# Linear attention's scores two levels at a time in mid-chunk, and its outputs in a lane of their own

## The chip, the cores and the metric

The kernel runs on one core of a Trainium2 chip. The time is that of one execution on the device, in microseconds. Five engines work side by side, each through its own queue of instructions in order: TensorE (PE in the profile, its weight loads PEld), VectorE (DVE), ScalarE (ACT), GpSimd (POOL) and SyncE (SP), which starts the DMAs. TensorE writes to PSUM, which here is two pools of four banks.

## The reference

Two layers of an encoder over 256 tokens and 16 learned meta tokens in front, width 2048. Each layer makes one large projection of the stream (6176 columns), two groups of attention heads from it, an output projection, a layer norm, a squared-ReLU MLP (width 8192) and a second layer norm. The meta tokens are dropped from the output.

The part that the change touches is the four heads of gated linear attention (query and key width 128, value width 256). Its recurrence, in each of the two directions, is

```
S_t = diag(a_t) S_{t-1} + k_t^T v_t        o_t = q_t S_t        log a_t = gate <= 0
```

and the head's output is normalised by its own mean square, scaled, and multiplied by SiLU of a gate that is also projected from the stream. The eight pairs of heads of neighbourhood attention, over a 4 x 64 grid with a window, a learned bias and the meta tokens as further keys, are interleaved with it.

## The kernel before, in words

*The stream of projections.* Everything large is a matmul with weights from HBM. A weight tile of 128 x 1024 is fetched (`raw`), rounded to fp32r on ScalarE (`wh`, L147) and its remainder is made by one subtraction on VectorE (`wl`, L148), so that two fp32r numbers stand for one fp32 number; the activations are kept in two parts as well. `three` (L151 on) makes each product of three matmuls, or of two where the right operand's halves lie side by side. `by_m` makes one output chunk of 128 columns at a time: 16 steps over the width, weights for 8 steps per tile, so a chunk takes two weight tiles. Weights are asked for one tile ahead, and `raw`, `wh` and `wl` have three buffers each.

*Where the small work goes.* The small work of the mixers is written as Python generators. They stand in two lanes, `fg` and `bg`. After every weight tile, that is in the middle and at the end of each output chunk, `by_m` calls `pump`, which lets the generators run on: one step of `fg`, and so many steps of `bg` as a credit allows. The credit grows by `GLA_R` = 1.3 per pump while the gates' eight chunks are projected, and by `GLA_NA` = 1.1 while the neighbourhood attention's 24 chunks are. The steps are issued behind the last weight's subtraction on its engine (`issue_after(self.wl)`), and the framework's scheduler sets the final order on each queue.

*Linear attention.* `gla_head` is one generator for one head; the four heads stand in `bg` one behind the other. The decay between two tokens is split by binary levels: at each level the sequence is cut in blocks, and the exponent is taken against the middle of the block, so that no exponent is positive. For each of the levels 7, 0, 1, ... 6, 8 `operands` makes four subtractions on GpSimd (L462), one exponential on ScalarE (L467) and one product with q and k on VectorE (L468). Then come the score matmuls: four of 64 x 64 (L497), for level 8 two of 128 x 128 (L492), and in the first layer one small one for the meta tokens (L500) at levels up to 4. The result is copied or written under a mask into `A`, `near` and `Am` (L503 to L518). `across` does the same for the meta tokens against all others (L522, L525). One level is made ready while the one before it is used; the levels' tile `lev` has three buffers. Then the same generator makes `am`, the output matmuls in two halves (L540 to L542), the mean square by two fp32r matmuls against a matrix of 1/256 (`mean`, L774), a Newton step for the inverse root (L432 to L434), and the normalised, gated outputs in two parts (L558, L559, `split`). Each head has 17 steps. The scores and outputs are plain fp32; projections and means are fp32r.

*Beside it.* `silu` makes the gates: the reciprocal on VectorE in two halves (L422), one per step, and the product in a third. `na_pair` is one generator per pair of attention heads in `fg`: it fetches the bias into `nb`, makes the scores (L599, L603), adds, softmaxes, transposes the values (L620, L621), then the probabilities (L635 to L638), and makes the outputs (L650, L655). After five of the six groups of attention projections `layer` runs `bg` empty and closes the pool of the linear attention.

*Banks.* Projections take PSUM banks from the pool `pm`, all the small work from `pb`.

Of the kernel before, what the change touches and what calls it, by code (L numbers as in the profile page):

```python
# [7 lines left out]
F32 = mybir.dt.float32  # L8
# [3 lines left out]
ALU = mybir.AluOpType  # L12
PSUM = bass.MemoryType.PSUM

P = 128
# [19 lines left out]
GLA_R, GLA_NA, NORMS = 1.3, 1.1, (1.0, 0.6)  # L35
# [12 lines left out]
class Trunk:  # L48
    def __init__(self, ctx, tc, ins, out):
        self.ctx, self.tc, self.nc = ctx, tc, tc.nc  # L50
        self.i, self.out = ins, out
        self.bg, self.fg, self.credit, self.fcredit = deque(), deque(), 0, 0
# [11 lines left out]
    def bank(self):  # L64
        return self.pb.tile([P, 512], F32, name="bg", tag="bg")
# [38 lines left out]
    def pump(self, fg, bg):  # L104
        self.fcredit += fg
        while self.fcredit >= 1:
            self.step(self.fg, 1)
            self.fcredit -= 1
        self.credit += bg
        while self.credit >= 1:  # L110
            self.step(self.bg, 1)
            self.credit -= 1

    def drain(self):
        while self.bg or self.fg:
            self.step(self.bg, 1)
            self.step(self.fg, 1)
# [72 lines left out]
    def by_m(self, acts, ns, evict, pump=(0, 0), apart=False, renew=False):  # L190

        nk = len(acts)
        for m, n in enumerate(ns):
            ps = self.pm.tile([P, 512], F32, name="mm", tag="mm")
            for k in range(nk):
# [3 lines left out]
                if k % 8 == 7 and k < nk - 1:  # L199
                    self.pump(*pump)  # L200
# [4 lines left out]
            self.pump(*pump)  # L205
# [16 lines left out]
    def layer(self, l):  # L222
# [4 lines left out]
        with ExitStack() as actx:  # L227
# [10 lines left out]
            if l:  # L238
                self.by_m(self.x, [L + 2] * 4, lambda m, ps: self.fixed(self.ev_k, m, ps), pump=(1, NORMS[0]),
# [9 lines left out]
            with ExitStack() as ectx:  # L249
                self.ep = pool("early", "right", ectx)  # L250
                self.fcredit = 0
                self.fg.append(self.gates())
                if l == 0:
                    self.by_m(self.x, [L] * 4, self.ev_v, pump=(1, 0))
                else:
                    for m, ps in enumerate(first):
                        self.ev_v(m, ps)
                self.by_m(self.x, [n] * 4, self.ev_q, pump=(1, 0))
                self.by_m(self.x, [L] * 4, lambda m, ps: self.ev_v(4 + m, ps), pump=(1, 0))
                self.drain()  # L260
            self.a2 = pool("na", "left", bufs=2)
            with ExitStack() as gctx:
                self.credit = 0
                self.g2 = pool("gla", "right", gctx, 2)
                for h in range(GH):
                    self.bg.append(self.gla_head(h))
                for g in range(2):
                    self.by_m(self.x, [n] * 4, lambda m, ps: self.ev_r(4 * g + m, ps), pump=(1, GLA_R))
                self.na_tiles()
                for g in range(6):  # L270
                    if g == 5:
                        while self.bg:
                            self.step(self.bg, 1)
# [3 lines left out]
                    self.by_m(self.x, ns, lambda m, ps: self.ev_na(4 * g + m, ps), pump=(1, GLA_NA))  # L277
# [140 lines left out]
    def silu(self, c, s, r):  # L418
        yield
        half = self.n // 2  # L420
        for p in (slice(0, half), slice(half, self.n)):
            self.nc.vector.reciprocal(s[:, p], s[:, p])  # L422
            yield
# [12 lines left out]
    def gla_head(self, h):  # L436
        nc, n, full, g2 = self.nc, self.n, self.full, self.g2
        be, qk = self.be[h], self.qk[h]
        bf, eb = be[:, 0, :], be[:, 1, :]
        A = g2.tile([P, 6, P], F32, name="A", tag="A")  # L440
        near = g2.tile([P, 2, 64], F32, name="near", tag="near")
        Am = g2.tile([NM, L], F32, name="Am", tag="Am")
        level = lambda: g2.tile([P, 2, L], F32, name="lev", tag="lev", bufs=3)

        def flat(t):

            return t.rearrange("p a c -> p (a c)")

        def operands(lv):
            if lv == 0:  # L450
                q2 = level()[:, 1, :]
                nc.gpsimd.tensor_scalar(q2[:, :n], qk[:, 1, :n], 2.0, 0.0, ALU.mult, ALU.add)
                return q2, flat(qk)
            w = L if full and lv <= 4 else T
            B, hb = 1 << lv, 1 << (lv - 1)
            nb = w // B
            t = level()
            v = lambda a: a[:, :w].rearrange("p (b h) -> p b h", h=B)
            f, e, tq, tk = v(bf), v(eb), v(t[:, 1, :]), v(t[:, 0, :])
# [7 lines left out]
            nc.scalar.activation(t[:, :, :w], t[:, :, :w], AF.Exp, scale=1 / TAU)  # L467
            nc.vector.tensor_tensor(t[:, :, :w], t[:, :, :w], qk[:, :, :w], ALU.mult)  # L468
            return t[:, 1, :], flat(t)

        def across():
            t = level()
            bm, e0 = bf[:, L - 1:L], eb[:, 0:1]
            ts = nc.gpsimd.tensor_scalar
            ts(t[:, 1, :T], bf[:, :T], bm, 1.0, ALU.subtract, ALU.mult)
            ts(t[:, 0, T:L], bf[:, T:L], bm, -1.0, ALU.subtract, ALU.mult)
            ts(t[:, 1, T:L], eb[:, T:L], e0, -1.0, ALU.subtract, ALU.mult)
            ts(t[:, 0, :T], eb[:, :T], e0, 1.0, ALU.subtract, ALU.mult)
            nc.scalar.activation(t, t, AF.Exp, scale=1 / TAU)
            nc.vector.tensor_tensor(t[:, 1, :n], t[:, 1, :n], qk[:, 1, :n], ALU.mult)  # L480
            nc.vector.tensor_tensor(t[:, 0, :], t[:, 0, :], qk[:, 0, :], ALU.mult)
            return t

        order = (7, 0, 1, 2, 3, 4, 5, 6, 8)
        ahead = operands(order[0])
        for at, lv in enumerate(order):
            q, k = ahead
            ahead = operands(order[at + 1]) if at + 1 < len(order) else across()
            ps = self.bank()
            for s in range(2):  # L490
                if lv == 8:
                    nc.tensor.matmul(ps[:, s * P:s * P + P], lhsT=k[:, s * P:s * P + P],  # L492
                                     rhs=q[:, P - s * P:T - s * P], start=True, stop=True)
                    continue
                for b in range(2):
# [525 lines left out]
```

## Time and profile before

| what | value |
|---|---|
| median of 3 runs | 2424.95 us (2424.75 to 2425.05) |
| the profiled execution's own time | 2424.98 us |
| its span, first to last instruction | 2423.2 us |
| granted TensorE clock | 0.997 |
| busy: PE / DVE / ACT / POOL | 2392.5 / 1575.1 / 1191.2 / 290.6 us |
| DMA | 417 MB, mean 172 GB/s |

The profile describes one execution. A line such as `L497 PE MATMUL bg<-lev 128*64 128x64 f32 x448` names the source line, the engine, the operation, the tile written and the tiles read, the part of the array that is used (rows * columns), the moving operand's shape, and how many there were. A plain fp32 matmul of the program appears as two in the profile. Numbers behind a bar are busy time, mean duration in ns, and the engine's idle time just before with what ended it. A row of the waits says who waited for whom: us in total, how often, the longest. A row of the timeline gives start and duration in us; matmuls overlap, so the distance between two starts says more of their price than the durations do. A row of windows gives the stretch, its length, busy time and number of instructions of PE, PEld, DVE, ACT and POOL, the clock, the DMA share and GB/s.

### The profile page before, as it was taken

The numbers are of one execution on the slowest core, as the hardware profiler recorded it, in microseconds if no ns is written. First come the engines' busy times: TensorE is split into PE (matmuls) and PEld (weight loads), VectorE is DVE, ScalarE is ACT, GpSimd is POOL, SyncE is SP. The second block draws the span as 40 slices with busy tenths as digits, with TensorE's granted clock in tenths as the row PEclk, the third lists the DMA queues.
The fourth block names the chain that finished last, engine by engine and source line by source line (L and its number), as shares of the span: only waits on it lengthen the run. The fifth ranks groups of instructions, "written<-read, shape, count | busy, mean of one in ns | idle before, by whom it ended". The sixth has DMA issues, their size and how long they took to land.

```text
span 2423.2 us, 43590 instructions
## 1 busy us (share of the span) xinstructions
PE 2392.5 (99%) x17532; PEld 2259.4 (93%) x17532; DVE 1575.1 (65%) x2481; ACT 1191.2 (49%) x1978; POOL 290.6 (12%) x447
## 2 busy tenths in 40 slices
PE   9999999999999999999999999999999999999997
PEld 8999999999999999999999889999988888888886
DVE  6678777775544455546577787778866555666655
ACT  6555555564433344444456555555644333444443
POOL 1165320010000000000020444300200000000000
PEclk9999999999999999999999999999999999999998
DMA  7544445555555555555546445446556555665553
GB/s 240 166 131 152 141 138 157 174 175 178 174 177 175 174 174 174 174 175 174 175 168 187 146 146 158 145 155 192 184 190 187 188 190 185 189 188 186 188 188 129
DMA packets 118361, 417.26 MB, mean 172 GB/s; under 512 B 13388, under 2 KB 16460, under 8 KB 118160
## 3 DMA queue, kind: packets, MB, share of 16 engines
q1 hardware_dynamic: 118160, 414.49, 54.6%
q8 instruction: 137, 2.24, 0.4%
q14 instruction: 64, 0.52, 0.1%
HBM read 412.34 MB, written 2.10 MB: 171 GB/s over the span
## 4 chain that ended last, share of the span: by engine, by line
PE 93%; DVE 3%; POOL 1%; issue 1%; ACT 1%; DMA 0%; SPq 0%; ACTq 0%; POOLq 0%; DVEq 0%
PE mm L156 22%; PE mm L160 17%; PE mm L162 17%; PE mm L161 17%; PE mm L157 11%; PE mm L186 5%; POOL lev L462 1%; DVE wl L148 1%; PE bg L497 1%; DVE acc L866 1%; PE bg L650 1%; PE bg L599 0%; PE bg L540 0%; PE bg L323 0%; PE bg L541 0%
## 5 line engine op out<-in xcount | busy, mean ns | idle before, releaser
L148 DVE TENSOR_TENSOR wl<-raw,wh 128x1024 fp32r<-128x1024 f32 (+1 forms) x772 | 946.9, 1227 | 656.0 <-ACT wh L147 646.4
L147 ACT CAST wh<-raw 128x1024 fp32r<-128x1024 f32 (+1 forms) x772 | 805.2, 1044 | 952.0 <-PE mm L161 403.5
L160 PE MATMUL mm<-x,wh 128*128 128x272 f32 (+2 forms) x2176 | 632.3, 291 | 0.0
L162 PE MATMUL mm<-x,wl 128*128 128x272 f32 (+2 forms) x2176 | 628.0, 289 | 0.0
L161 PE MATMUL mm<-x,wh 128*128 128x272 f32 (+2 forms) x2176 | 627.8, 288 | 0.0
L160 PEld LDWEIGHTS mm<-x,wh 128*128 128x128 f32 x2176 | 412.7, 190 | 3.2 <-issue 0.4
L162 PEld LDWEIGHTS mm<-x,wl 128*128 128x128 f32 x2176 | 410.1, 188 | 0.3
L156 PE MATMUL mm<-x,wh 128*128 128x512 f32 x1152 | 409.5, 397 | 0.0
L161 PEld LDWEIGHTS mm<-x,wh 128*128 128x128 f32 x2176 | 409.4, 188 | 0.0
L157 PE MATMUL mm<-x,wl 128*128 128x256 f32 x1152 | 324.6, 282 | 0.4 <-DVE wl L148 0.4
L156 PEld LDWEIGHTS mm<-x,wh 128*128 128x128 f32 x1152 | 217.5, 189 | 50.8 <-issue 0.4
L156 PE MATMUL mm<-y,wh 128*128 128x512 f32 x704 | 247.9, 393 | 0.0
L157 PEld LDWEIGHTS mm<-x,wl 128*128 128x128 f32 x1152 | 217.3, 189 | 1.3 <-DVE wl L148 1.1
L162 PE MATMUL mm<-y,wl 128*128 128x272 f32 x704 | 203.1, 288 | 0.0
L160 PE MATMUL mm<-y,wh 128*128 128x272 f32 x704 | 203.0, 288 | 0.0
L161 PE MATMUL mm<-y,wh 128*128 128x272 f32 x704 | 202.7, 288 | 0.0
L157 PE MATMUL mm<-y,wl 128*128 128x256 f32 x704 | 197.5, 281 | 0.5 <-DVE wl L148 0.5
L156 PE MATMUL mm<-u,wh 128*128 128x512 f32 x512 | 180.6, 393 | 0.0
L462 POOL TENSOR_TENSOR lev<-be 128x128 f32<-128x128 f32 (+1 forms) x256 | 162.1, 663 | 108.2 <-ACT gt L337 26.9
L156 PEld LDWEIGHTS mm<-y,wh 128*128 128x128 f32 x704 | 131.8, 188 | 30.0
L160 PE MATMUL mm<-u,wh 128*128 128x272 f32 x512 | 147.7, 288 | 0.0
L162 PE MATMUL mm<-u,wl 128*128 128x272 f32 x512 | 147.7, 288 | 0.0
(242 smaller groups left out, 3291.0 us busy)
## 6 DMA issues: line engine op xcount, KB each, us to landing
raw<-in_wff SPq DMA_DIRECT2D x512, 512.0 KB, 3.6
raw<-in_win SPq DMA_DIRECT2D x190, 512.0 KB, 3.6
raw<-in_wout SPq DMA_DIRECT2D x64, 512.0 KB, 3.6
nb<-in_nab SPq DMA_DIRECT2D x16, 352.0 KB, 3.6
out<-acc SPq DMA_DIRECT2D x8, 256.0 KB, 2.2
xraw<-in_xT SPq DMA_DIRECT2D x7, 272.0 KB, 5.7
wraw<-in_wup SPq DMA_DIRECT2D x2, 392.0 KB
raw<-in_win SPq DMA_DIRECT2D x4, 128.0 KB, 2.9
```

What stands on the lines that cost most here:

```text
L147: nc.scalar.copy(wh[:, c], raw[:, c])
L148: self.wl = nc.vector.tensor_tensor(wl[:, c], raw[:, c], wh[:, c].bitcast(F32), ALU.subtract).ins
L156: mm(ps, lhsT=wh[:, c:c + P], rhs=x.both[:, :, :T], start=first, stop=False)
L157: mm(ps[:, T:], lhsT=wl[:, c:c + P], rhs=xh[:, :T], start=False, stop=last)
L160: mm(o, lhsT=wh[:, c:c + P], rhs=xh[:, :n], start=first, stop=False)
L161: mm(o, lhsT=wh[:, c:c + P], rhs=xl[:, :n], start=False, stop=False)
L162: mm(o, lhsT=wl[:, c:c + P], rhs=xh[:, :n], start=False, stop=last)
L186: self.nc.tensor.matmul(ps[m][:, :n], lhsT=parts[p][0][:, c:c + P], rhs=acts[j][parts[p][1]][:, :n], start=j + p == 0, stop=j == nk - 1 an ...
L462: tt = lambda o, x, y: nc.gpsimd.tensor_tensor(o, x, y, ALU.subtract)
L497: nc.tensor.matmul(ps[b * 64:b * 64 + 64, s * 64:s * 64 + 64], lhsT=k[:, c:c + 64], rhs=q[:, r:r + 64], start=True, stop=True)
L650: nc.tensor.matmul(r[hs], lhsT=(v2 if rest else v1)[:, t, hs], rhs=p2[:, t, :] if rest else p1[:, 2 * t + hh, :], start=rest, stop=not rest)
L866: return self.nc.vector.tensor_tensor(v, v, by[:, None, :].to_broadcast([P, m, n]), alu)
```

## The change

One generator, `gla`, takes the place of the four `gla_head`s for the scores. It goes through 20 steps, five for each head: the levels (7, 0), (1, 2), (3, 4), (5, 6), and (8, 9), where 9 is what `across` did. A step's operands, made one step ahead across heads too, lie in one tile of twice the size with two buffers; where both levels have the same width, one exponential and one product serve both. Both levels' scores lie in one PSUM bank; (8, 9) takes two banks.

After its last scores a head's `gla_out` is put into a new lane, `late`. It makes both halves of the output in one step and both halves of the normalisation in one step. While it runs, the next head's scores go on in `bg`.

`pump` now takes three numbers, and `by_m` a pair of them, for the middle and for the end of a chunk. Among the mixers they are (1, 1, 1) and (1, 0, 1): scores in the middle only, the other two lanes at both places, `late` first, then scores, then `fg`. The fractional credits are gone. Banks for the mean and for the value transposes come from the projections' pool there (`bank(beside)`).

Smaller edits: `silu` makes its second half and the product in one step; the attention bias is fetched straight into the tile `ns` that takes the sum, and its layout in HBM is ordered to suit (done on the host); `na_pair` has one more empty step ahead of the transposes of the probabilities; `layer` empties `bg` and `late` together.

```diff
-    def pump(self, fg, bg):
-        self.fcredit += fg
-        while self.fcredit >= 1:
-            self.step(self.fg, 1)
-            self.fcredit -= 1
+    def pump(self, fg, bg, late=0):
+        self.step(self.late, late)
+        if not self.beside:
+            self.step(self.fg, fg)
         self.credit += bg
         while self.credit >= 1:
             self.step(self.bg, 1)
             self.credit -= 1
+        if self.beside:
+            self.step(self.fg, fg)
...
                 if k % 8 == 7 and k < nk - 1:
-                    self.pump(*pump)
+                    self.pump(*pump[0])
...
-            self.pump(*pump)
+            self.pump(*pump[-1])
...
-                for h in range(GH):
-                    self.bg.append(self.gla_head(h))
+                self.bg.append(self.gla())
+                self.beside, mixers = True, ((1, 1, 1), (1, 0, 1))
...
-        level = lambda: g2.tile([P, 2, L], F32, name="lev", tag="lev", bufs=3)
+        t = self.g2.tile([P, 2, 2, L], F32, name="lev", tag="lev")
...
+        w = wide(levels[0])
+        if wide(levels[1]) == w and levels[1]:
+            decay(t[:, :, :, :w], w, qk[:, None, :, :w].to_broadcast([P, 2, 2, w]))
+        else:
+            decay(t[:, 0, :, :w], w, qk[:, :, :w])
...
+        steps = [(h, p) for h in range(GH) for p in ((7, 0), (1, 2), (3, 4), (5, 6), (8, 9))]
+        ahead = self.operands(*steps[0])
+        yield
+        for at, (h, levels) in enumerate(steps):
+            now = ahead
+            if at + 1 < len(steps):
+                ahead = self.operands(*steps[at + 1])
...
+                self.late.append(self.gla_out(h, A, Am))
+                yield
+                continue
+            for i, (lv, (q, k)) in enumerate(zip(levels, now)):
+                p2, pm = ps[:, i * P:i * P + P], ps[:64, T + i * NM:T + i * NM + NM]
+                for s in range(2):
+                    for b in range(2):
+                        c, r = (s * P + x * 64 for x in (b, b if lv < 7 else 1 - b))
+                        nc.tensor.matmul(p2[half[b], s * 64:s * 64 + 64], lhsT=k[:, c:c + 64], rhs=q[:, r:r + 64],
+                                         start=True, stop=True)
...
             nc.scalar.activation(sq[:, e, :n], o, AF.Square)
             os_.append(o)
-            yield
         nc.vector.tensor_tensor(sq[:, 0, :n], sq[:, 0, :n], sq[:, 1, :n], ALU.add)
-        ms = yield from self.mean(sq[:, 0, :n], GDV, pool=g2)
+        ms = yield from self.mean(sq[:, 0, :n], GDV, pool=g2, beside=True)
...
-        bias = b.tile([P, 4, NKEY], F32, name="nb", tag="nb")
-        nc.sync.dma_start(bias, self.i["nab"][self.l, c])
         s = b.tile([P, 4, NKEY], F32, name="ns", tag="ns")
+        nc.sync.dma_start(s, self.i["nab"][self.l, c])
...
-        pv = self.bank()
+        pv = self.bank(beside=True)
```

182 lines of the change are left out of this document (90 added, 92 removed).

## The prediction

> **What bounds the kernel now.** I read the page first: the span, the busy shares and the shares of the chain.
>
> ```profile
> span 2423.2 us, 43590 instructions
> PE 2392.5 (99%) x17532; PEld 2259.4 (93%) x17532; DVE 1575.1 (65%) x2481; ACT 1191.2 (49%) x1978; POOL 290.6 (12%) x447
> PE 93%; DVE 3%; POOL 1%; issue 1%; ACT 1%; DMA 0%; SPq 0%; ACTq 0%; POOLq 0%; DVEq 0%
> ```
>
> TensorE is busy for 99% of the span and makes 93% of the chain. So only two things can move the time: what TensorE spends on its instructions, and how long it stands waiting. I read the second from the waits of PE over the whole run, of which these are three rows; the fourth is from the same view of the second layer's mixers (1340 to 1605 us) alone:
>
> ```profile
> PE bg L497 <- DVE lev L468: 1.6, 2, 1.3
> ...
> PE mm L157 <- DVE wl L148: 0.9, 2, 0.5
> ...
> PE bg L492 <- DVE lev L468: 0.2, 1, 0.2
> ...
> PE mm L157 <- DVE wl L148: 0.4, 1, 0.4
> ```
>
> Eight rows name the mixers' own matmuls (the score, output and attention lines L492 to L650). They run from the 1.6 of the first to the 0.2 of the last, and sum to 5.6 us. One of the two waits for a weight's low half (L157) lies among the mixers too, the fourth row's 0.4. That makes 6.0 us of 2423: the most that the removal of every wait could bring.
>
> The first thing, the price of an interruption, is not in the mean durations, because matmuls overlap. It is in the distances between starts, so I read the timeline of PE around single bursts, where a few small matmuls of a mixer stand in the stream of projection matmuls. First one level of scores, as it stands alone:
>
> ```profile
> 119.06 0.29 PE L162 MATMUL mm<-x,wl 128*128 128x272 f32 x1
> 119.28 0.45 PE L497 MATMUL bg<-lev,qk 128*64 128x64 f32 x8
> 119.56 0.24 PE L500 MATMUL bg<-lev,qk 128*64 128x16 f32 x2
> 119.73 0.39 PE L160 MATMUL mm<-x,wh 128*128 128x272 f32 x1
> 119.96 0.29 PE L161 MATMUL mm<-x,wh 128*128 128x272 f32 x1
> ```
>
> Then two levels that happened to fall together, then two fp32r matmuls of a mean:
>
> ```profile
> 126.39 0.29 PE L162 MATMUL mm<-x,wl 128*128 128x272 f32 x1
> ...
> 127.64 0.29 PE L161 MATMUL mm<-x,wh 128*128 128x272 f32 x1
> ```
>
> ```profile
> 157.46 0.29 PE L162 MATMUL mm<-x,wl 128*128 128x272 f32 x1
> 157.59 0.41 PE L774 MATMUL bg<-sp,onesr 128*128 128x272 f32 x2
> ...
> 157.96 0.29 PE L161 MATMUL mm<-x,wh 128*128 128x272 f32 x1
> ```
>
> I measure a burst from the start of the projection matmul before it to the start of the second one behind it, because that one is still late (0.23 behind the first where 0.13 is usual), and take off the two usual steps, 2 x 0.125. One level: 119.96 - 119.06 - 0.25 = 0.65 us. Two levels together: 127.64 - 126.39 - 0.25 = 1.00, where two alone cost 1.30. So leaving the projection's format for plain fp32 and coming back costs 0.30 us, whatever is in between. The two fp32r matmuls cost 157.96 - 157.46 - 0.25 = 0.25, two usual steps: no entry price at all.
>
> **The change part by part.** Its matmuls are the same ones (900 between the projections in both built programs); only their grouping differs. In the built order I count the bursts between projection matmuls: 173 before, 151 after.
>
> *Scores in pairs.* Each head has nine levels and the meta step, ten fp32 groups; they become five. Over 4 heads and 2 layers, 40 groups lose their own entry. For 32 of them (levels with levels) that is 0.30 each, 9.6 us. The other 8 put the last level with the meta step, both 128 x 128. Such a group alone:
>
> ```profile
> 189.55 0.29 PE L162 MATMUL mm<-x,wl 128*128 128x272 f32 x1
> 189.68 0.61 PE L492 MATMUL bg<-lev 128*128 128x128 f32 x4
> 190.25 0.29 PE L161 MATMUL mm<-x,wh 128*128 128x272 f32 x1
> ```
>
> It costs 0.45 us (190.25 - 189.55 - 0.25) for four passes that move twice what a level's pass moves; its entry is not to be read apart and lies between 0.20 and 0.30. I take 0.25: 8 x 0.25 = 2.0. Together 11.6 us.
>
> *What shared a burst already.* Before, 1.1 to 1.3 steps per pump often fell beside an attention step, and the entry was then shared already. How much that saves depends on the pair:
>
> ```profile
> 208.07 0.29 PE L162 MATMUL mm<-x,wl 128*128 128x272 f32 x1
> 209.47 0.29 PE L161 MATMUL mm<-x,wh 128*128 128x272 f32 x1
> ...
> 293.23 0.29 PE L162 MATMUL mm<-x,wl 128*128 128x272 f32 x1
> 295.08 0.29 PE L161 MATMUL mm<-x,wh 128*128 128x272 f32 x1
> ...
> 319.17 0.29 PE L162 MATMUL mm<-x,wl 128*128 128x272 f32 x1
> 321.01 0.29 PE L161 MATMUL mm<-x,wh 128*128 128x272 f32 x1
> ...
> 358.99 0.29 PE L162 MATMUL mm<-x,wl 128*128 128x272 f32 x1
> 360.54 0.29 PE L161 MATMUL mm<-x,wh 128*128 128x272 f32 x1
> ...
> 244.64 0.29 PE L162 MATMUL mm<-x,wl 128*128 128x272 f32 x1
> 246.46 0.29 PE L161 MATMUL mm<-x,wh 128*128 128x272 f32 x1
> ...
> 163.75 0.29 PE L162 MATMUL mm<-x,wl 128*128 128x272 f32 x1
> 164.58 0.28 PE L161 MATMUL mm<-x,wh 128*128 128x272 f32 x1
> ```
>
> These are six bursts by their two ends; the last is a level without its meta part, 0.58 us alone. The attention scores (L599) alone cost 1.15 (208.07 to 209.47); with a level 1.60 (293.23), against 1.15 + 0.65 = 1.80 apart: 0.20 saved. With a 128-wide group 1.59 (319.17), against 1.15 + 0.45 = 1.60: nothing saved, since the change of the array's shape inside the burst costs what the entry did. The attention outputs (L650) alone cost 1.30 (358.99); with a level without its meta part 1.57 (244.64), against 1.30 + 0.58: 0.30 saved; with a meta part 0.25; I take 0.28. In the built order before there are six pairs of levels (6 x 0.30), six L599 with a level (6 x 0.20), seven L650 with a level (7 x 0.28) and eight pairs with a 128-wide group (nothing): 1.8 + 1.2 + 2.0 = 5.0 us that the change gives up. After, six bursts hold scores and attention outputs (6 x 0.28 = 1.7), and one step is split in two (-0.3). Transposes have no part in this: in the timeline they share nothing with a level, nor lose by it.
>
> Sum of TensorE's own work: 11.6 - 5.0 + 1.7 - 0.3 = 8.0 us less. Bounds: 6.9 if every shared pair were worth more by 0.05 and the 128-wide entry 0.20; 9.0 the other way.
>
> [...]
>
> *Waits.* This is the term that the trace of before does not show. All scores now come once per output chunk, in its middle, and a step's differences, exponentials and products are twice as long. GpSimd may begin a pair as soon as the buffer of the pair two steps before is read, so a pair has two chunks, some 14 us, from there to its use. Its eight subtractions take 8 x 0.67, the exponential is twice 0.66 and the product 1.28, some 8 us:
>
> ```profile
> L462 POOL TENSOR_TENSOR lev<-be 128x136 f32<-128x136 f32 (+1 forms) x96 | 61.5, 669 | 28.1 <-PE bg L500 10.9 <-PE bg L497 8.8 <-DVE lev L468 6.7
> L467 ACT ACTIVATE lev<-lev 128x544 f32<-128x544 f32 x16 | 10.5, 658 | 29.0 <-POOL lev L462 29.0
> L758 DVE TENSOR_TENSOR acc<-acc,cs 128x1088 f32<-128x1088 f32 x2 | 2.6, 1284 | 0.0
> ```
>
> So the score matmuls' own waits (1.6 and the like) should mostly go. What comes late next is the weight's low half, because VectorE gets tighter:
>
> ```profile
> 113.00:309.00 196.00, 193.98 (x1722) 185.58 (x1721) 154.16 (x311) 110.56 (x245) 104.61 (x162) 1.00 0.45 141
> L148 DVE TENSOR_TENSOR wl<-raw,wh 128x1024 fp32r<-128x1024 f32 x66 | 82.6, 1253 | 22.8 <-ACT wh L147 20.4 <-PE bg L603 2.2
> L422 DVE RECIPROCAL rs<-rs 128x136 f32<-128x136 f32 x16 | 15.8, 991 | 3.1 <-POOL rs L413 3.0
> L514 DVE COPY_PREDICATED near<-mask,bg 128x128 f32<-128x128 uint8 x24 | 6.9, 286 | 0.4 <-DVE Am L518 0.4
> ```
>
> In that stretch VectorE (the third sum of the windows row) was busy 154 of 196 us, 79%. After, all 20 score steps stand in the first 21 chunks instead of up to chunk 28, the gates' reciprocals keep pace with their chunks instead of trailing, and the output lane lies beside. A gate chunk has 2 x 1.25 of weights, 2 x 0.99 of reciprocals, 1.28 of product and 2 x 0.29 of masks, 6.3 us without the smaller copies, in a chunk of 48 x 0.125 + 1.0 = 7.0 us on TensorE. Once per head the built order puts 14 instructions between two weight subtractions (the two reciprocals, the Newton step, both halves' normalisation, the masks), about 6.4 us with 0.4 for each that is no reciprocal, against a tile of 3 us. Weights are kept up to two tiles ahead (three buffers), 6 us, so this place is about met, not clearly hidden. Queued behind it on VectorE is the next low half, and TensorE waits for that. I put 0.9 us, the two waits of that row of before together, on each of the 8 heads: 7.2 us of waits after, in place of 6.0. Bounds: none (0), and per head the whole 3.6 us by which 6.4 + 1.25 exceeds a tile with its burst (29 us).
>
> *Edits at no cost.* The attention's bias now lands in the tile that takes the sum: its DMA must wait until that buffer's transposes of two pairs earlier are done, six chunks back, and the 16 of them stand in SP's queue among the weights' DMAs as before; uncovered, one would hold back the next weight behind it, by the 3.6 us that such a transfer takes to land:
>
> ```profile
> nb<-in_nab SPq DMA_DIRECT2D x16, 352.0 KB, 3.6
> ```
> The mean's and the value transposes' banks come from the projection's four; each is read over one chunk before its turn comes again, and uncovered would stop the next projection matmul for one read, of the mask copy's order (0.29 us). The extra pause before the attention's transposes delays outputs that are wanted chunks later. One product and one exponential in place of two each save those engines the start of an instruction; that only eases their queues, and I count nothing.
>
> *Sum.* The profiled execution took 2424.98 us (span 2423.2), the median is 2424.95: 2425.0 - 8.0 + 7.2 - 6.0 = 2418.2 us, 0.28% faster.
>
> **The rivals.** (1) The saving is real but VectorE's lateness takes about all of it: waits between 9 and 19 us after, time 2420 to 2430, say 2424. For: VectorE's 6.3 of 7.0. Against: in the whole run before, a low half made an L157 matmul wait only twice. (2) Slower: the place once per head is met with one tile of lead instead of two, because the step before has used the other; each head then stops for up to 3.6 us. It decides from (8.0 + 4.85 + 6.0)/8 = 2.4 us per head on; at 3.6 the time is 2425 - 8.0 + 29 - 6 = 2440. Against: the gates' reciprocals fall away after the eighth chunk, so three of four heads have it easier. (3) The price belongs to the array's shape, not to the format: 6.0 saved instead of 8.0, 2420.2 with the same waits, no change that can be told. (4) The waits go altogether, 2411.
>
> **How the numbers follow.** A difference under 0.2%, 4.85 us, can't be told from none. Faster needs less than 9.2 us of waits after (6.0 + 8.0 - 4.85), or 7.2 in case (3). I give my forecast with case (4) 0.60, of which (4) has 0.1; case (1) with (3) 0.26, of which (3) has 0.06; case (2) 0.14. The range runs from case (4), 2411, to 2430, the top of case (1); beyond lies most of case (2), and little below.
>
> **What would show it.** Right: the two-level burst in the middle of a chunk costs 1.0 us by the same distances; 151 bursts; PE's score lines wait less; PE's span in the mixers (113 to 385 us, 1348 to 1605 us) shorter by 3 to 4 us each. Wrong: waits of the projection matmuls for the low half above 9 us, or a burst of two levels that costs 1.3. The parts behind the mixers must not move.

## The result, and the profile after

The changed kernel takes 2461.4 us (median of four runs, 2459.5 to 2463.5) against 2424.9 for the kernel before: a ratio of 1.0151, 95% interval 1.0133 to 1.0169. It is slower by 36.5 us, where 6.8 less were forecast. Its profiled execution took 2460.09 us. The page's lines that answer to those of before:

```profile
span 2458.2 us, 43462 instructions
PE 2400.1 (98%) x17532; PEld 2267.9 (92%) x17532; DVE 1568.0 (64%) x2457; ACT 1187.4 (48%) x1954; POOL 270.6 (11%) x447
PE 86%; DVE 3%; POOL 3%; issue 1%; ACT 1%; ACTq 0%; POOLq 0%; DVEq 0%
```

TensorE made 93% of the chain before and makes 86% now; GpSimd (POOL) went from 1% to 3%. Where the time is lost is seen in windows over the two layers' mixers, first of the kernel before, then of after (stretch, length, busy time of PE, PEld, DVE, ACT, POOL, granted clock, DMA share, GB/s):

```profile
113.00:385.00 272.00, 269.15 (x2370) 258.40 (x2369) 209.55 (x441) 152.43 (x357) 117.06 (x181) 1.00 0.46 142
1348.00:1605.00 257.00, 253.73 (x1981) 229.03 (x1979) 204.95 (x374) 151.12 (x334) 110.44 (x188) 1.00 0.48 148
```

```profile
113.00:385.00 272.00, 257.25 (x2229) 247.41 (x2227) 195.68 (x404) 141.71 (x322) 101.31 (x176) 0.97 0.42 133
1348.00:1605.00 257.00, 238.33 (x1816) 214.47 (x1815) 189.22 (x346) 138.40 (x287) 94.10 (x173) 0.98 0.44 138
```

TensorE stood idle for 2.9 + 3.3 = 6.1 us among the mixers before, and for 14.8 + 18.7 = 33.4 after. The granted clock, 1.00 before, is 0.97 and 0.98. VectorE is *less* busy in both stretches, because the work is spread over a longer time: it is no fuller than it was. I also compared the start of the n-th weight cast on ScalarE in both traces: after runs 16.0 us behind at 425 us and still 16.0 behind at 1338, then 34.7 behind from 1689 us to the end. So all of the loss lies in the mixers. Within the first mixers the lag is 22 us at 281 us, about where after's scores end, and falls to 16 by 425.

Which waits these are, from the waits of PE in after (us in total, how often, the longest):

```profile
PE bg L800 <- ACT sp L212: 11.5, 4, 3.9
PE bg L676 <- DVE p L666: 5.1, 3, 2.5
PE mm L166 <- DVE wl L152: 4.6, 5, 1.7
PE mm L161 <- DVE wl L152: 4.5, 4, 2.1
PE bg L624 <- DVE y L213: 3.9, 2, 2.4
PE bg L569 <- ACT rv L419: 1.9, 1, 1.9
```

The largest is the mean's matmul (L800), which waits for ScalarE's cast of the sum of squares (`sp`). The timeline at one of the four, from 205 us (start, duration, instruction; the brackets give the idle time before it and what ended it):

```profile
205.14 5.00 POOL L462 TENSOR_TENSOR lev<-be 128x136 f32<-128x136 f32 x8 [0.45 <-PE bg L537]
```

```profile
207.68 0.38 ACT L570 ACTIVATE sq<-bg 128x272 f32<-128x272 f32 x1
207.96 0.24 ACT L543 COPY A<-bg 64x128 f32<-64x128 f32 x1
210.17 1.11 ACT L469 ACTIVATE lev<-lev 128x1088 f32<-128x1088 f32 x1 [1.97 <-POOL lev L462]
211.19 0.40 ACT L212 CAST sp<-sq 128x272 fp32r<-128x272 f32 x1
```

```profile
209.20 0.65 DVE L572 TENSOR_TENSOR sq<-sq 128x272 f32<-128x272 f32 x1
211.31 1.29 DVE L470 TENSOR_TENSOR lev<-lev,qk 128x1088 f32<-128x1088 f32 x1 [1.14 <-ACT lev L469]
212.52 0.44 DVE L213 TENSOR_TENSOR sp<-sq,sp 128x272 fp32r<-128x272 f32 x1
```

```profile
207.91 0.29 PE L166 MATMUL mm<-x,wl 128*128 128x272 f32 x1
211.64 0.39 PE L800 MATMUL bg<-sp,onesr 128*128 128x272 f32 x1 [3.44 <-ACT sp L212]
...
213.01 0.39 PE L800 MATMUL bg<-sp,onesr 128*128 128x272 f32 x1 [0.27 <-DVE sp L213]
```

The sum of squares was ready at 209.85 and its cast takes 0.40. But the next pair's exponential (L469) stands ahead of the cast in ScalarE's queue, and waits for GpSimd's eight subtractions, which took 5.00 us. ScalarE stands idle for 1.97 us, the cast comes 1.34 us late, its low half on VectorE behind the pair's product comes later still, and TensorE waits 3.44 + 0.27 us. Only 1.34 of the 3.44 us are this exponential's, though: TensorE came to the matmul at 208.20, 1.65 us before the sum itself was ready. At the wait of 3.23 us at 1461.96 the same count gives 1.99. At the longest, 3.92 us at 1414.20, it gives nothing, because the sum came last, behind a weight's subtraction on VectorE that took 2.62 us beside GpSimd's eight subtractions, where 1.22 is usual:

```profile
1413.18 3.03 POOL L462 TENSOR_TENSOR lev<-be 128x128 f32<-128x128 f32 x8
```

```profile
1414.67 2.62 DVE L152 TENSOR_TENSOR wl<-raw,wh 128x1024 fp32r<-128x1024 f32 x1
```

```profile
1417.66 0.40 ACT L212 CAST sp<-sq 128x256 fp32r<-128x256 f32 x1 [0.36 <-DVE sq L572]
```

At the fourth, 0.94 us at 165.15, the cast stands ahead of the next exponential. So the place behind the exponential is directly worth 3.3 of these waits' 11.8 us; the rest has other paths. Then there is a second price:

```profile
205.00:213.00 8.00, 4.30 (x31) 3.86 (x31) 6.13 (x12) 6.01 (x18) 5.00 (x8) 1.00 0.42 134
213.40:216.80 3.40, 3.40 (x17) 3.40 (x17) 3.08 (x10) 1.08 (x3) 0.00 (x0) 0.50 0.38 107
```

In the 3.4 us behind the wait TensorE is granted half its clock, and a projection matmul takes 0.227 us in place of 0.125. I count six such stretches in after, none in the mixers of before; the excess of their steps sums to 9.1 us.

The account: 27.3 us more of idle time and 9.1 of half clock, less 8.0 of TensorE's own work, make 28.4; 35.1 are to be explained between the two profiled executions. The other 6.7 us I can't assign to a row.

### The profile page after: what moved, and what is told of

Its sections match the earlier page's. It is cut to its first block, busy times and chain, and to the rows that moved or that the text cites. A ratio compares the mean times of both kernels' runs of the same rounds, so it can differ in the third digit from the quotient of the medians.

```text
span 2458.2 us, 43462 instructions
## 1 busy us (share of the span) xinstructions
PE 2400.1 (98%) x17532; PEld 2267.9 (92%) x17532; DVE 1568.0 (64%) x2457; ACT 1187.4 (48%) x1954; POOL 270.6 (11%) x447
## 4 chain that ended last, share of the span: by engine, by line
PE 86%; DVE 3%; POOL 3%; issue 1%; ACT 1%; ACTq 0%; POOLq 0%; DVEq 0%
PE mm L160 21%; PE mm L164 15%; PE mm L166 15%; PE mm L165 15%; PE mm L161 11%; PE mm L190 5%; POOL lev L462 2%; DVE wl L152 1%; DVE acc L892 1%; PE bg L676 1%; PE bg L624 1%; PE bg L534 0%; DVE lev L470 0%; ACT wh L151 0%; ACT lev L469 0%
## 5 line engine op out<-in xcount | busy, mean ns | idle before, releaser
L166 PE MATMUL mm<-x,wl 128*128 128x272 f32 (+2 forms) x2176 | 632.2, 291 | 4.7 <-DVE wl L152 4.6
L166 PEld LDWEIGHTS mm<-x,wl 128*128 128x128 f32 x2176 | 413.8, 190 | 6.0 <-DVE wl L152 5.8
L161 PE MATMUL mm<-x,wl 128*128 128x256 f32 x1152 | 325.3, 282 | 4.0 <-DVE wl L152 3.9
L161 PEld LDWEIGHTS mm<-x,wl 128*128 128x128 f32 x1152 | 218.0, 189 | 5.3 <-DVE wl L152 5.2
L166 PE MATMUL mm<-y,wl 128*128 128x272 f32 x704 | 203.1, 288 | 0.0
L161 PE MATMUL mm<-y,wl 128*128 128x256 f32 x704 | 197.5, 281 | 0.6 <-DVE wl L152 0.6
L164 PE MATMUL mm<-u,wh 128*128 128x272 f32 x512 | 147.7, 288 | 0.0
L166 PE MATMUL mm<-u,wl 128*128 128x272 f32 x512 | 147.7, 288 | 0.0
L165 PE MATMUL mm<-u,wh 128*128 128x272 f32 x512 | 147.5, 288 | 0.0
```

The lines of the kernel that those rows point to most:

```text
L161: mm(ps[:, T:], lhsT=wl[:, c:c + P], rhs=xh[:, :T], start=False, stop=last)
L164: mm(o, lhsT=wh[:, c:c + P], rhs=xh[:, :n], start=first, stop=False)
L165: mm(o, lhsT=wh[:, c:c + P], rhs=xl[:, :n], start=False, stop=False)
L166: mm(o, lhsT=wl[:, c:c + P], rhs=xh[:, :n], start=False, stop=last)
```

## The experiments

The expectations speak of these theories. A: the pair's exponential stands in ScalarE's queue ahead of GpSimd's unfinished subtractions (first as a matter of two buffers instead of three, then, as A', whatever the buffers). B: the mean stands one pump behind the outputs, before it stood two. C: VectorE has too much to do in these chunks. D: the subtractions cost by running beside VectorE's work. Medians, and ratios to the kernel before with 95% intervals:

| kernel | us | ratio |
|---|---|---|
| after | 2461.4 | 1.0151 (1.0133 to 1.0169) |
| e1 three pair buffers | 2473.2 | 1.0196 (1.0179 to 1.0213) |
| e2 mean a pump later | 2455.9 | 1.0128 (1.0113 to 1.0143) |
| e3 both | 2472.0 | 1.0195 (1.0179 to 1.0210) |
| e4 pairs in one lane | 2443.4 | 1.0076 (1.0061 to 1.0091) |
| e5 no subtractions | 2410.6 | 0.9942 (0.9927 to 0.9956) |
| e6 single levels | 2431.5 | 1.0028 (1.0018 to 1.0039) |
| e7 exponential a pump later | 2463.3 | 1.0163 (1.0146 to 1.0180) |
| e8 e7 and mean later | 2447.5 | 1.0093 (1.0078 to 1.0108) |
| e9 exponential not waiting | 2473.9 | 1.0200 (1.0183 to 1.0218) |
| e10 subtractions ahead | 2430.7 | 1.0022 (1.0013 to 1.0032) |
| e11 e10 and mean later | 2427.2 | 1.0009 (1.0000 to 1.0018) |
| e12 e9 with subtractions paced | 2446.8 | 1.0091 (1.0076 to 1.0106) |
| e13 e11, scores at 0.8 per chunk | 2424.0 | 0.9997 (0.9987 to 1.0007) |
| e14 e11, gate's addition on ScalarE | 2419.9 | 0.9979 (0.9970 to 0.9988) |
| e15 e10 in one lane | 2432.2 | 1.0033 (1.0021 to 1.0044) |
| e16 e14 at 0.8 per chunk | 2418.6 | 0.9974 (0.9964 to 0.9984) |
| e17 before, gate's addition on ScalarE | 2424.5 | 0.9998 (0.9988 to 1.0008) |
| e18 after, gate's addition on ScalarE | 2452.4 | 1.0114 (1.0099 to 1.0129) |

### Buffers and the mean's place: e1, e2, e3

```diff
-        t = self.g2.tile([P, 2, 2, L], F32, name="lev", tag="lev")
+        t = self.g2.tile([P, 2, 2, L], F32, name="lev", tag="lev", bufs=3)     # e1, e3; am with one buffer
...
+        if beside:
+            yield                               # e2, e3: in mean, ahead of its bank
```

> Changed kernel with three pair buffers instead of two (the output's am tile has one instead of two, for the room). Theory A: GpSimd may not begin a pair before the pair two steps earlier has been read, so the pair's exponential waits for it at the head of ScalarE's queue (83.0 us in 31 waits, longest 4.3) and everything behind it is late; then the mean's 11.8 us of waits, the 5.8 us of L676 and L534 on p and the 3.9 us of L624 on y go mostly, and with them the half clock: 2415 to 2430 us. Theory B: the mean's matmuls simply stand one pump behind the outputs instead of two; then nothing of that moves: 2450 us or more. Theory C: VectorE has too much work in these chunks: 2450 us or more too.

> Changed kernel with one empty step of the output lane between the mean's casts and its matmuls, so that these stand two pumps behind the outputs, as before the change. Theory B: the 11.8 us of waits at L800 go, and the half clock behind them (some 6 us): 2440 us or a little less. Theory A: those waits go too, but the casts stay late and other waits (L676, L624, the low halves) stay or grow by some us: 2440 to 2450 us. Theory C: the wait moves to the low halves: 2455 us or more.

> Three pair buffers and the later mean together. Theory A: as with three buffers alone, within 4 us of it. Theory B: as with the later mean alone, within 4 us. If both causes are real and apart: about the 8.0 us that the fewer bursts save come out, 2415 to 2420 us.

A third buffer made it worse, 2473. PE's waits for the mean and ScalarE's for GpSimd in e1:

```profile
PE bg L800 <- ACT sp L212: 20.4, 6, 5.1
```

```profile
ACT lev L469 <- POOL lev L462: 103.4, 32, 6.3
```

With a buffer free earlier, the framework's scheduler put the exponentials earlier still; the longest wait grew to 6.3 us. In ScalarE's order most of them stand two weight casts earlier than in after. So too few buffers, the first form of A, is not it. (e1 also leaves `am` one buffer, and 5.7 us of TensorE's waits in it are for `am`, 0.2 in after; e10 below has one buffer too, and no such wait.) B is worth 5.5 us: in e2 the mean's waits fall from 11.8 us to 3.2, but others appear (5.6 us for a weight's high half, for one). Both together (e3) are no better than the third buffer alone.

### Which part of the change: e4, e6

```diff
-                self.beside, mixers = True, ((1, 1, 1), (1, 0, 1))
+                self.beside, mixers = True, ((1, 0.7, 0), (1, 0.7, 0))         # e4, with the next line
-                self.late.append(self.gla_out(h, A, Am))
+                yield from self.gla_out(h, A, Am)
...
-        steps = [(h, p) for h in range(GH) for p in ((7, 0), (1, 2), (3, 4), (5, 6), (8, 9))]
+        steps = [(h, p) for h in range(GH) for p in ((7,), (0,), (1,), (2,), (3,), (4,), (5,), (6,), (8,), (9,))]
+                self.beside, mixers = True, ((1, 1, 1), (1, 1, 1))             # e6, with the line above
```

> Scores in pairs, but the outputs again in the scores' lane, which gets 0.7 steps per pump at both places; the pairs lie in both halves of a chunk and up to the end of the attention chunks. Theory A (pairs with two buffers): the waits for GpSimd stay, 2445 us or more. Theory B (outputs beside the next head's scores, mean too near): outputs have the queues to themselves, 2425 us or less. Theory C: VectorE's work is spread over 28 chunks instead of 20, 2430 us or less.

> Single levels as before the change (ten steps per head, three buffers of one level, scores at both pumps of a chunk), with all else of the change kept: the outputs in their own lane beside the next head's scores, the mean one pump behind them. The levels' bursts cost their entry again: 8 us of TensorE's work come back. If pairs cause the waits (A'): the waits go back near the 6 us of before and the time is 2425 to 2430. If the lane beside the scores, and the density of VectorE's work that it brings, causes them (C): waits stay at 20 us and more, 2445 to 2460. If the mean's place does (B): the mean's waits stay at 10 us or more, 2440.

Single levels with all the rest of the change take 2431.5: the lane, the banks and the mean's new place cost 6.5 us together, and the pairs, which save 8, cost the other 30 net. Pairs without the second lane (e4) still take 2443. ScalarE's waits for GpSimd in the kernel before, in after and in e6:

```profile
ACT lev L467 <- POOL lev L462: 84.6, 51, 3.6
```

```profile
ACT lev L469 <- POOL lev L462: 83.0, 31, 4.3
ACT lev L484 <- POOL lev L454: 26.6, 8, 4.3
```

```profile
ACT lev L469 <- POOL lev L462: 81.9, 51, 3.7
```

With the meta step's rows (25.5 us in 8 waits before, 20.9 in 8 in e6) the sums are 110, 110 and 103 us: they are alike, and the sum is not what costs. In the rows of L462 the waits of after are fewer and longer than before, 2.7 us instead of 1.7 in the mean. But length alone does not explain it either: e4 has 104 us in 34 waits, 3.1 in the mean and 5.6 at most, and is 18 us faster than after. What stands behind a wait must matter too; no run varied the length alone.

### With GpSimd's work taken away: e5

```diff
+        nc.gpsimd.memset(t, 0.0)
         for i, lv in enumerate(levels):
             if lv:
-                differences(t[:, i], lv)
+                pass
```

> After, with GpSimd's subtractions for the decays replaced by one fill of the pair's tile with zeros: the decays are left out of the computation, exponentials and products stay. GpSimd then has one short instruction per pair in place of eight. If the lateness comes from the exponential standing in ScalarE's queue ahead of unfinished subtractions (theory A'): ScalarE's waits on GpSimd nearly vanish, the mean's wait and the other waits with them, no stretch at half clock remains among the mixers, 2417 to 2424 us. If VectorE simply has too much to do in these chunks (theory C, VectorE's work is unchanged here): the waits for the weights' low halves and for the mean stay, 2445 us or more. If the mean's place one pump behind the outputs is the cause by itself (B): about 2455 with the mean's wait still near 10 us.

2410.6 us. TensorE's waits, all rows but one of 0.2:

```profile
PE mm L190 <- ACT wh L151: 4.6, 2, 4.4
PE mm L190 <- DVE wl L152: 1.0, 1, 1.0
PE bg L859 <- DVE acc L763: 1.0, 1, 1.0
PE mm L161 <- DVE wl L152: 0.5, 1, 0.5
```

The first two lie at the starts of layers and the third in the norm behind the mixers; among the mixers 0.7 us is left at most. VectorE's work is all there, so C falls as a cause by itself; the mean stands one pump behind the outputs, so B falls as a cause by itself. Everything above 2411 needs GpSimd's subtractions. Which of their effects it is, e5 does not tell: it takes away the waits for them and their running beside VectorE (D) at once.

### Where they do the harm: e7, e8, e9, e12

e7 issues exponential and product one pump later than the subtractions; e8 adds e2's edit.

```diff
+            yield
+            finish()            # decay(...) of the next pair
             yield
```

> After, with the exponential and the product of the next pair issued one pump later than its subtractions (at the chunk's end; in the queue of ScalarE they now stand behind the mean's cast and the copies of the step's scores). Nothing is left out. A': ScalarE's waits on GpSimd fall from 83 us to below 40, the mean's cast is no longer behind them, the waits of TensorE fall by 15 us or more: 2430 to 2445. C: the time stays within 5 us of after's 2461. B: the mean's own wait stays, since it has no more distance than in after: 2450 to 2461.

> The same, and the mean one pump later too. A' with B as a second, smaller cause: 2425 to 2440, TensorE's waits among the mixers at 15 us or less and no stretch at half clock. C: within 5 us of 2456, what the later mean alone gave.

e7 was a miss: 2463. In ScalarE's queue the mean's cast now stood ahead of the exponential, but the waits for GpSimd remained, only with other work behind them:

```profile
ACT lev L469 <- POOL lev L462: 72.2, 29, 5.0
ACT lev L488 <- POOL lev L454: 30.7, 8, 4.5
```

103 us against 110. With the mean later too (e8) it is 88 us and 2447.5, still 22 above before and above the 2440 expected. So the place in the queue alone is not it either: what has to change is when GpSimd is done. e9 and e12 take the wait away and keep the load: the subtractions go into a tile that nothing reads, the exponential reads the gates' sums.

```diff
+        dif = self.g2.tile([P, 2, 2, L], F32, name="dif", tag="dif", bufs=1)     # subtractions write here
-            nc.scalar.activation(o, o, AF.Exp, scale=1 / TAU)
+            nc.scalar.activation(o, d, AF.Exp, scale=1 / TAU)                    # d: a slice of be
...
+            nc.vector.tensor_copy(seen, self.last[:, 0, 0, :1])                  # e12 alone, ahead of the next pair
```

> After, with GpSimd's subtractions all there and at their places, but into a tile of their own (128 x 1088, one buffer) that nothing reads; the exponential reads the gates' sums instead. So the decays are left out of the computation, GpSimd's load and its contention with VectorE stay, and only ScalarE's waiting for the subtractions is gone (am has one buffer, for room). If the wait in ScalarE's queue is the cause (theory A'): close to what the kernel without subtractions took, 2410 to 2418. If the subtractions cost by running beside VectorE (theory D: they lengthen its instructions or stand in its way): 2440 to 2460, as after.

> The kernel whose exponential doesn't read the subtractions again, with GpSimd kept from running ahead: VectorE copies one column of a pair's subtractions (128 x 1) before the next pair's may overwrite them, so that the subtractions keep after's pace and the gates' own instruction on GpSimd does not stand behind several heads of them. The decays are left out of the computation as there. A' (ScalarE's wait is the cause): 2412 to 2425. D (what is left of the cost is GpSimd's work beside VectorE's): 2440 or more. If it falls between, at what the subtractions issued ahead took (2431), the last 16 to 20 us above 2411 belong to GpSimd's presence and not to ScalarE's wait.

Both missed A's number, and showed the second half of the mechanism. In e9 GpSimd, bound by nothing, ran its subtractions far ahead, and its one instruction for a gate (1 + exp, L417) stood behind them. VectorE's reciprocals waited for that, with the weights' low halves queued behind them. VectorE's wait and TensorE's:

```profile
DVE rs L425 <- POOL rs L417: 69.1, 11, 18.2
```

```profile
PE mm L161 <- DVE wl L152: 27.1, 3, 13.7
PE mm L166 <- DVE wl L152: 27.1, 2, 13.8
```

Five waits of TensorE make 54 of its 63 us above 2411. Paced (e12), the same wait is 35.6 us, longest 4.7, and the time 2446.8. Two of TensorE's three long waits for the mean there (2.72 us at 171.47, 2.83 at 1411.82) follow such a wait of VectorE, of 2.5 us each; the third (2.47 us at 1454.80) follows a VectorE instruction that took 3.17 us in place of 0.69 beside eight subtractions, which is D. So it isn't ScalarE's wait alone: an engine that queues behind GpSimd's subtractions pays, ScalarE through the exponential or VectorE through the gate, and now and then one that runs beside them.

### Subtractions a step earlier: e10, e11

```diff
+        dif = self.g2.tile([P, 2, 2, L], F32, name="dif", tag="dif", bufs=1)     # and am with one buffer
...
             if at + 1 < len(steps):
-                ahead = self.operands(*steps[at + 1])
+                ahead = finish()                                # exponential lev<-dif, product
+            if at + 2 < len(steps):
+                finish = self.operands(*steps[at + 2])          # subtractions into dif
```

> Nothing is left out. The subtractions of a pair go into a tile of their own (one buffer) and are issued one step earlier than in after, two steps ahead of the scores; exponential and product write the pair's tile from it, at their old places. So GpSimd may work on the next pair as soon as the exponential has read the last one and need not wait for the score matmuls to free a buffer: a chunk of 7 us more. A': ScalarE's waits on GpSimd fall from 110 us to below 40 and the time to 2412 to 2425; with the mean's place as a second cause up to 2430. D: 2450 or more.

> The same, and the mean one pump later. If the mean's place matters by itself (B): 3 to 10 us less than the kernel before it. If it was only hurt by ScalarE's lateness: within 2 us of it.

```profile
ACT lev L476 <- POOL dif L462: 10.5, 6, 3.4
ACT lev L488 <- POOL dif L454: 7.8, 8, 3.2
```

ScalarE's waits fall from 110 us to 18, and the time by 30.7 us to 2430.7, with nothing left out and GpSimd's load as before. So the largest single cause is when the subtractions are done: in after they can start only when score matmuls free a pair's buffer, and the exponential is reached before they are through. The order in ScalarE's queue is not what was repaired: the mean's cast stands right behind an exponential for six of the eight heads in e10, for three in after. The time, 2430.7, is just above the 2430 expected at most. The mean's place is worth another 3.4 us.

### The last part: e13 to e18

```diff
-        nc.gpsimd.tensor_scalar(s, s, 1.0, 1.0, ALU.mult, ALU.add)
+        nc.scalar.activation(s, s, AF.Identity, bias=self.one)                  # e14, e16, e17, e18
...
-                self.beside, mixers = True, ((1, 1, 1), (1, 0, 1))
+                self.beside, mixers = True, ((1, 0.8, 1), (1, 0, 1))            # e13, e16
```

> Subtractions ahead and the mean later, and scores at 0.8 steps per chunk in place of 1, so that the 20 steps spread over 25 chunks. Nothing is left out. C (what is left is VectorE's and ScalarE's density): 5 to 10 us less than 2427, so 2417 to 2422, and faster than before. If density plays no part: 2425 to 2430.

> Subtractions ahead and the mean later, and the gates' one addition (1 + exp, 16 instructions on GpSimd, behind which VectorE's reciprocal waits) moved to ScalarE. Nothing is left out. If GpSimd's queue is what is left: VectorE's waits for it (8 us per layer) go, 3 to 8 us less than 2427. If not: within 2 us of it, or more by ScalarE's longer queue.

> Subtractions ahead with the outputs back in the scores' own lane at 0.7 steps per pump, as in the kernel with one lane (2443), whose scores and outputs don't run beside each other. Nothing is left out. If the lane beside the scores causes what is left: 2412 to 2422. If the two causes are the same one seen twice: 2427 to 2431, no better than two lanes.

> Subtractions ahead, the mean later, the gate's addition on ScalarE, and scores at 0.8 steps per chunk. Nothing is left out. The 3 us of the slower pace and the 7 of the gate's addition add up: 2414 to 2418. If they are the same wait removed twice: 2419 to 2421.

> The kernel before, with the gate's addition on ScalarE and nothing else. If the gain of the repaired kernels over the kernel before belongs to the pairs, this is within 2 us of 2425; if it belongs to the gate's addition, 2418 to 2421.

> After, with the gate's addition on ScalarE and nothing else. If the gates behind GpSimd are a cause of their own: 5 to 10 us less than 2461, 2451 to 2456. If they hurt only where the subtractions run ahead (there is little of VectorE's waiting for them in after, 3.7 us): within 2 us of 2461.

Taking the gate's addition out of GpSimd's queue is worth 7.3 us with the subtractions ahead (e14) and 9.0 in after itself (e18), where VectorE's own wait for it is only 3.7 us in sum; there the waits of ScalarE fell too, from 110 us to 93, which fits subtractions that no longer share GpSimd with it. In the kernel before the same edit is worth 0.5 us, no difference (e17). The slower pace brings 3.2 us without the gate's edit (less than the 5 to 10 expected of density) and 1.3 with it, within the intervals of e14 and e16: that the waits they remove are partly the same fits, but is not shown. The second lane is no cause once the subtractions are ahead: without it (e15) it is 2432, no better. ScalarE waits 73 us for GpSimd there and 18 in e10, at nearly the same time, so once more the sum of these waits does not set the time.

e16, with all four edits, is the fastest kernel that computes everything: 2418.6 us, 0.26% below the kernel before (interval 0.16% to 0.36%). Its mixers by the same windows:

```profile
113.00:385.00 272.00, 271.24 (x2422) 263.67 (x2421) 208.57 (x431) 157.99 (x352) 106.12 (x178) 1.00 0.44 145
1348.00:1605.00 257.00, 253.06 (x1994) 230.03 (x1994) 197.98 (x352) 150.77 (x325) 98.76 (x170) 0.99 0.45 149
```

Idle 0.8 + 3.9 us in place of 33.4. Its time can't be told from e14's. The 8 us between it and the kernel without subtractions are not settled; contention between GpSimd and VectorE (D) may be in them. For the slowdown itself D is small by the traces: VectorE's instructions among the mixers exceed the medians of their groups by 8.5 us in sum in after and by 11.6 in before; the one at 1414.67 is the only one in after that is over by more than 0.7 us.

## Why the prediction was wrong

*TensorE's own work: right, as far as the runs show.* The 151 bursts were counted in the built order before any run; a burst of two levels in the middle of a chunk reads:

```profile
127.95 0.29 PE L166 MATMUL mm<-x,wl 128*128 128x272 f32 x1
...
128.97 0.40 PE L164 MATMUL mm<-x,wh 128*128 128x272 f32 x1
129.20 0.28 PE L165 MATMUL mm<-x,wh 128*128 128x272 f32 x1
```

129.20 - 127.95 - 0.25 = 1.00 us, as foretold. e5 fits the whole term: with all waits gone, 2425.0 - 8.0 - 6.0 = 2411.0 was rival (4)'s time, 2410.6 was found. Rival (3), 6.0 us saved (the 8.0 without the 8 x 0.25 = 2.0 of the merges with a 128-wide group), would have given 2413.0; e5's medians lie nearer 8.0, though its interval does not exclude the other. So whether the 0.30 us of an entry belong to the number format or to the array's shape no run shows.

*The waits: wrong.* The step that failed is the term "7.2 us of waits after, in place of 6.0" and its bounds of 0 to 29. By e5, everything above 2411 is waiting and what follows from it: 50 us, more than the upper bound. That bound was built for one mechanism, VectorE's place once per head. The low halves' waits (L161 and L166) did come to 9.1 us, just over the mark I had set for them, but with VectorE's work unchanged e5 has 0.5: they were late from elsewhere.

*The sentence under it* that went astray was that a pair has "two chunks, some 14 us" for "some 8 us" of work, so that the score matmuls' waits should mostly go. That is true, and they did: no row of the linear attention's scores stands among the large waits. The pair whose subtractions began at 205.14 was ready at 212.60, and its scores came only at 225.30. But I asked only whether the pair is ready for its scores, not what stands behind the exponential in ScalarE's queue, and behind the product in VectorE's, while they wait for GpSimd: the mean's cast, `am`, the attention's copies, the weights' casts and low halves. The row of before that I quoted had this in it, 29.0 us of ScalarE's idle time before L467 put down to POOL; the prediction gave it no price.

*Edits at no cost: partly wrong.* That the mean stands one pump behind the outputs was not costed; it is worth 3.4 to 5.5 us. Among TensorE's waits nothing is seen of the attention bias's DMA or of the projections' banks.

*The clock* was left out of the sum altogether. Its 9 us are a price on top of long waits.

*Rivals and checks.* Rival (2) had the side and a price of 2440 but the wrong mechanism. The mixers, foretold shorter by 3 to 4 us each, are longer by 16.0 and 18.7. The parts behind them did not move, as foretold. e16's 2418.6 lies next to the forecast's 2418.2, but that is partly luck: e16 has four edits that the forecast did not have, and its waits are not the ones that the 7.2 us stood for. It does show that a kernel with the change's pairs can be faster than before once GpSimd is ready in time, which in the change it was not.

## What to carry to other kernels

When a change makes an engine's instructions longer or batches them, ask for each of them not only whether its result is in time, but what stands behind it in its own queue while it waits for its input; idle time before an instruction on a half-busy engine is free only as long as nothing behind it is urgent. A slow engine that serves two others, as GpSimd did here (0.39 us for a subtraction of 136 columns, where VectorE takes 1.22 for one of 1024), can be relieved by letting it start earlier into a tile of its own, which was worth 31 us here where a third buffer of the final tile (with one buffer fewer for another) cost 12. And leaving the suspected work out altogether (e5) told in one run how much there was to win, before any repair was tried.

## What was not expected of the hardware

*Half a clock after a wait.* In the six stretches of half clock in after the granted clock is 0.50 for 3.41 us (five of them) or 6.83 (the second). They begin at 213.39, 261.17, 288.48, 1418.29, 1442.18 and 1466.08 us. Each begins within 1.7 us of the end of a wait of TensorE: 3.44 us from 208.20 and 0.27 from 212.74; 2.39 from 259.02, which still had 0.24 us to run when the half clock began; 2.45 from 284.37; 3.92 from 1414.20; 0.66 from 1435.41 and 1.72 from 1439.36; 3.23 from 1461.96. Each stretch cost 1.1 to 2.3 us in longer steps, together 9.1 us on top of some 18 us of waits. Not every wait had this price: behind 1.92 us from 157.92, 2.01 from 1530.41, and 0.95 and 2.05 close together from 1395.77 the clock stayed at 1.00. So the sum of neighbouring waits alone does not tell which are followed by half clock, 0.66 + 1.72 being less than 0.95 + 2.05. What does is not shown here.

*Plain GpSimd instructions stretched beside VectorE.* The same subtraction takes 0.4 us alone and 1.4 beside a weight's subtraction. From the timeline of after, two on their own, then the third, which meets VectorE's:

```profile
195.03 0.78 POOL L462 TENSOR_TENSOR lev<-be 128x136 f32<-128x136 f32 x2 [2.23 <-PE bg L518]
```

```profile
195.77 1.41 POOL L462 TENSOR_TENSOR lev<-be 128x136 f32<-128x136 f32 x1
```

```profile
195.68 1.22 DVE L152 TENSOR_TENSOR wl<-raw,wh 128x1024 fp32r<-128x1024 f32 x1 [1.45 <-ACT wh L151]
```

The third alone took 1.41 us where the two took 0.78, and it ended 0.28 us after VectorE's. At 1414.67 it was VectorE's instruction that was long, 2.62 us where 1.22 is usual: it began while GpSimd's eight were running (1413.18 to 1416.21) and ended at 1417.29, while the eight took 3.03 us, no more than 8 x 0.39 = 3.12. So a pair's eight subtractions, 3.1 us at 0.39 each, took 5.00 us at 205, and their end is hard to foretell for whatever is queued behind them. Why now the one and now the other is lengthened is not shown.
